# A hybrid layer with product-key experts: all picks of a group before their transposes, and longer leads in the written order

## The chip, the cores and the metric

The kernel runs on one core of a Trainium2 chip. The time is device microseconds (us) of one execution. Below, PE is the tensor engine (PEld its weight loads), DVE the vector engine, ACT the scalar engine, POOL the general engine, SP the engine that issues most DMAs.

## The reference

One layer on 1024 tokens of width 1024, in float32:

```python
h = rmsnorm(x, norm_mix_g)
hq, hf, hi, hg, cb, cc, ch, gates = split(h @ w_in)
# HGRN2: a gated linear recurrence, 8 heads x 64, chunks of 64 tokens
#   S_t = diag(f_t) S_(t-1) + k_t v_t^T ;  o_t = S_t^T q_t ;  k_t = 1 - f_t
y_a = rmsnorm_per_head(o) * hg_out_norm_g * silu(hg)
y_b = cb * causal_depthwise_conv3(cc * ch)
merged = sigmoid(g_a) * (y_a @ w_branch_hg) + sigmoid(g_b) * (y_b @ w_branch_conv)
x = x + merged @ w_out
# PEER: 8 heads, each the 16 best of 128 x 128 experts by two lists of 128 keys
q = rmsnorm(x) @ w_query
v1, i1 = top_k(q[:, :, 0] . keys1, 16);  v2, i2 = top_k(q[:, :, 1] . keys2, 16)
top_s, pos = top_k(v1 + v2, 16);  idx = (i1 * 128 + i2)[pos];  gate = softmax(top_s)
x = x + sum_k gate * gelu(peer_u[idx] . h) * peer_v[idx]
out = rmsnorm(x)
```

## The kernel before

The 1024 tokens are 8 tiles of 128, and the tiles are mixed in five groups: 0, 1, then 2 and 3, 4 and 5, 6 and 7. For each group `front` (L494) transposes the normalised input and makes the convolution branch, `recurrence` (L557) goes through four pairs of heads, `gates_a` and `gates_b` make the merge gates, and `post` (L606) merges, multiplies by `w_out`, takes the second norm (L646), transposes its result on PE (`transpose_whole`, L260, copied out by ACT at L261), multiplies by `w_query` (the loop with L251 and L665) and finds the best 16 keys of each half. `picks_of` (L685) then calls `pick` (L820) for each tile: the best 16 of the candidates (`top16`), the softmax, and the numbers of the experts (an equality, a product and a sum per head, L865, L867, L868).

The experts are computed in two ways. Tiles 0, 1, 6 and 7 fetch their rows of `peer_u` and `peer_v` one by one with indirect DMAs issued by POOL (L913); each row costs DVE one pass (L943 for u, L949 for v, called row operations below). Tiles 2 to 5 go through a dense phase, in which PE multiplies with all experts (L287, L290, L1068, L278 to L280; DVE L239, L1043, L1079): for these tiles `pick` ends with an integer conversion (L882) and three PE transposes (L886) whose results ACT copies out, and `all_gates` (L968) spreads the gates over all 16384 experts ahead of the dense phase (DVE L1007, L1010, PE L987, ACT L991, L1015; a *spread*).

The recurrence of one pair of heads: a scan on DVE (L573), differences of its levels on POOL (L704, L708), exponentials on ACT (L710), products on DVE (L718, L719), then in `chunks` (L724) for each tile 28 small matmuls of scores (L739, L741; *score matmuls*) with one transpose (L744), the masks on DVE (L749, L757), and two *state steps*, each with matmuls at L764, L768, L770 and the new state on DVE (L775). A matmul at L787 for the output norm ends a pair.

The written order of all this is decided ahead of time. `together` (L387) holds these generators and always runs the one that has done the smallest share of its total, by a clock that counts modelled matmul time; a `yield` with a number makes a generator sleep for that many units, so other generators' work is written ahead of what comes behind it. These numbers stand in one line (L67): LEV lies between the products and the score matmuls, GRAM between score matmuls and the first state step, STATE between state steps, NORM between the norm and its transposes, PICK between L882 and the transposes at L886. A scheduler then settles the order on each engine; on the chip each engine runs its list strictly in that order and waits on semaphores. So a `yield` costs no time by itself: it chooses what stands ahead of a wait.

The row operations enter by `paced`, one step of rows (two of u, two of v) each 7 units of that clock while the mixing goes on, and by `interleave` in the dense phase, which spreads the steps that are left over it.

Of the kernel before, what the change touches and what calls it, by code (L numbers as in the profile page):

```python
# [23 lines left out]
P = 128  # L24
# [39 lines left out]
T_GB, T_FIRST = 27, 40.0  # L64
ROW_STEPS, T_DENSE = 290, 1305.0

LEV, GRAM, STATE, MERGE, NORM, PICK, SPREAD, OUT = 11.55, 1.944, 0.864, 4.752, 3.24, 50.0, 2.592, 3.24  # L67


def zipped(a, b, every):  # L70
# [55 lines left out]
class Layer:  # L126
# [61 lines left out]
    def place_picks(self, q):  # L188

        r, M, at = self.ring, types.SimpleNamespace(), self.M.big[q]  # L190
        M.top_kb, M.topi_kb = at, at + 2
        M.pr, M.cu, M.fi, M.ci = r(at + 4, 1.625), r(at + 5.625, 1), r(at + 4, 1), r(at + 7.25, 1.625)
        M.cv, M.eq, M.tvp = r(at + 8.875, 1.625), r(at + 8.875, 1.625), r(at + 10.5, .5, 2)
        M.gt, M.pf, M.xf = r(at + 11.5, .5), r(at + 12, .5), r(at + 12.5, .5)
        M.xu, M.i12 = r(at + 13, 1), r(at + 14, 1)
        return M

    def place_dense(self):
# [486 lines left out]
    def picks_of(self, G):  # L685

        while self.posted < G.no:
            yield 1
        for t in range(G.n // P):
            yield from self.pick(G.n0 // P + t, G.top[:, t], G.topi[:, t], G.mem)  # L690
        self.picked = G.no

    def decays(self, qs, k, b):
# [126 lines left out]
    def pick(self, tile_no, top, topi, mem):  # L820

        nc = self.nc
# [22 lines left out]
        if for_gather:  # L845
            gate = self.picks.tile([P, HEADS, TOPK], F32, tag=f"gate{tile_no}", name="gate")
        else:
            gate = mem.gt.take([HEADS, TOPK])
# [22 lines left out]
        xf, gate = (z.rearrange("p h k -> p (h k)") for z in (xf, gate))  # L871
# [6 lines left out]
        xu, i12 = mem.xu.take([2, PICKS], U32), mem.i12.take([2, PICKS])  # L878
# [1 line left out]
        nc.vector.tensor_scalar(xu[:, 1], xu[:, 0], NKEYS - 1, None, op0=ALU.bitwise_and)  # L880
        nc.vector.tensor_scalar(xu[:, 0], xu[:, 0], 7, None, op0=ALU.logical_shift_right)
        nc.vector.tensor_copy(i12, xu)  # L882
        yield PICK
        ps = self.ps()
        for i, src in enumerate((i12[:, 1], i12[:, 0], gate)):
            self.tc.keep_in_program_order(nc.tensor.transpose(ps[:, i * P:(i + 1) * P], src, self.ident))  # L886

# [1 line left out]
        at = self.M.pt_kb + 2 * DENSE.index(tile_no)  # L889
        keys, gate, beyond = self.view(at, [P, 2, 2], F16), self.view(at + 1, [P]), self.view(at + 1.5, [P, 2], F16)  # L890
# [6 lines left out]
                                upper.unsqueeze(2).broadcast_to([P, P, 2]), op=ALU.subtract)  # L897
        pt = keys, gate, beyond
        self.pt[tile_no] = pt
        yield  # L900


    def gather(self, tiles):
# [290 lines left out]
```

## Time and profile before

| | before |
|---|---|
| median of 3 runs | 3154.16 us (3154.1 to 3157.51) |
| profiled execution | 3154.26 us, its span 3152.5 us |
| PE busy | 2844.1 us, 90% of the span |
| DVE busy | 2592.4 us, 82% |
| ACT busy | 1236.9 us, 39% |
| POOL busy | 1444.8 us, 46% |
| mean granted TensorE clock | 0.94 |

The span is the time from the first to the last instruction; the execution's time is 1.8 us longer. The shares are averages over stages: from 1850 us to the end lies the dense phase in full speed, before it the mixing.

### The profile page before, as it was taken

What the parts mean: (1) busy time and instruction counts of PE and PEld (TensorE: products, weight loads), DVE (VectorE), ACT (ScalarE), POOL (GpSimd) and SP (SyncE); (2) the same over time, 40 slices, a digit from 0 to 9 for tenths busy, and PEclk for the clock granted to TensorE, in tenths of its full rate; (3) what the DMA queues carried; (4) which work ended last, traced back from release to release, by engine and by line L of the source; (5) the groups of instructions that cost most, each with busy time, mean ns of one, the idle gap of its engine ahead of it and who ended that gap; (6) DMA issues with size and microseconds to landing.
All of it is one profiled execution on the core that took longest, in us unless ns stands there. A gap on an engine that the chain in (4) does not pass through costs nothing.

```text
span 3152.5 us, 45726 instructions
## 1 busy us (share of the span) xinstructions
PE 2844.1 (90%) x15988; PEld 2423.3 (77%) x15988; DVE 2592.4 (82%) x5706; ACT 1236.9 (39%) x2241; POOL 1444.8 (46%) x1328
## 2 busy tenths in 40 slices
PE   8899789998998988456686999999999999999998
PEld 7898678877887777345575878888888888888886
DVE  3347467887799979987879999998888989888888
ACT  3632633332333567356662333332333333333332
POOL 0102444466543632553625454555555546455442
PEclk9999799999999999777798999999999999999999
DMA  8588688989887897878798888999999989999986
GB/s 288 199 281 289 226 303 317 329 294 357 313 316 276 318 344 277 288 251 295 270 374 287 305 309 323 369 363 332 339 340 342 345 296 370 344 346 332 337 303 239
DMA packets 336135, 979.08 MB, mean 311 GB/s; under 512 B 30881, under 2 KB 107169, under 8 KB 333857
## 3 DMA queue, kind: packets, MB, share of 16 engines
q0 software_dynamic: 147456, 536.94, 47.4%
q1 hardware_dynamic: 188448, 439.23, 38.8%
q8 instruction: 126, 2.06, 0.2%
q14 instruction: 105, 0.85, 0.1%
HBM read 929.90 MB, written 46.14 MB: 310 GB/s over the span
## 4 chain that ended last, share of the span: by engine, by line
PE 56%; DVE 14%; ACT 6%; DMA 3%; issue 3%; POOL 3%; DVEq 0%; POOLq 0%; ACTq 0%
PE ps L1068 17%; PE ps L287 14%; PE ps L290 7%; PE ps L251 7%; DVE mem_g L949 3%; DVE mem_g L943 2%; PE ps L278 2%; PE ps L280 2%; PE ps L279 2%; PE ps L632 2%; ACT mem_y L1015 1%; ACT mem_a L991 1%; DMA mem_a<-in_peer_u,idx 1%; PE ps L739 1%; DVE mem_o L1007 1%
## 5 line engine op out<-in xcount | busy, mean ns | idle before, releaser
L251 PE MATMUL ps<-mem_h,mem_w 128*128 128x256 f32 (+1 forms) x4480 | 858.5, 350 | 17.2 <-ACT mem_h L261 11.3
L251 PEld LDWEIGHTS ps<-mem_h,mem_w 128*128 128x128 f32 x4480 | 741.9, 199 | 97.1 <-ACT mem_h L261 12.2
L913 POOL DMA_INDIRECT mem_g<-in_peer_v,idx x320 | 399.5, 1248 | 475.8 <-DVE mem_g L943 180.6
L913 POOL DMA_INDIRECT mem_g<-in_peer_u,idx x329 | 399.7, 1215 | 447.0 <-DVE mem_g L949 138.7
L1068 PE MATMUL ps<-mem_v,mem_ph 128*128 128x512 f32 x2304 | 567.2, 396 | 12.2 <-ACT mem_ph L238 12.2
L1068 PEld LDWEIGHTS ps<-mem_v,mem_ph 128*128 128x128 f32 x2304 | 433.3, 188 | 118.6 <-ACT mem_ph L238 13.1
L287 PE MATMUL ps<-mem_ht,mem_s 128*128 128x512 f32 x2048 | 510.1, 391 | 9.4 <-DVE mem_ht L239 7.3
L287 PEld LDWEIGHTS ps<-mem_ht,mem_s 128*128 128x128 f32 x2048 | 386.2, 189 | 92.5 <-DVE mem_ht L239 8.0
L943 DVE SCALAR_TENSOR_TENSOR mem_g<-mem_g 128x1024 f32<-128x1024 f32 x329 | 405.3, 1236 | 27.4 <-DMA mem_g<-in_peer_u,idx 25.2
L949 DVE SCALAR_TENSOR_TENSOR mem_g<-mem_g 128x1024 f32<-128x1024 f32 x320 | 412.3, 1288 | 17.7 <-DMA mem_g<-in_peer_v,idx 16.2
L238 ACT ACTIVATE mem_s<-mem_raw 128x512 fp32r<-128x512 f32 x256 | 161.4, 632 | 588.7 <-PE ps L287 555.7
L913 POOL DMA_INDIRECT mem_e<-in_peer_v,idx x150 | 196.3, 1309 | 193.1 <-DVE mem_g L949 167.3
L290 PE MATMUL ps<-mem_ht,mem_s 128*128 128x512 f32 x1024 | 275.6, 391 | 0.0
L913 POOL DMA_INDIRECT mem_e<-in_peer_u,idx x134 | 175.9, 1313 | 162.6 <-DVE mem_e L943 131.2
L239 DVE TENSOR_TENSOR mem_s<-mem_raw,mem_s 128x512 fp32r<-128x512 f32 x256 | 176.3, 691 | 72.7 <-PE ps L290 45.8
L290 PEld LDWEIGHTS ps<-mem_ht,mem_s 128*128 128x128 f32 x1024 | 193.3, 189 | 40.5
L238 ACT ACTIVATE mem_v<-mem_z 128x1024 fp32r<-128x1024 f32 x128 | 129.2, 1054 | 209.9 <-PE ps L280 196.3
L949 DVE SCALAR_TENSOR_TENSOR mem_g<-mem_e,mem_g 128x1024 f32<-128x1024 f32 x150 | 191.7, 1278 | 0.4
L704 POOL TENSOR_TENSOR mem_y<-mem_y 128x128 f32<-128x128 f32 (+1 forms) x120 | 59.9, 499 | 269.2 <-DVE mem_y L573 240.5
L1015 ACT ACTIVATE mem_y<-mem_o,mem_z 128x128 f16<-128x128 f16 x512 | 156.2, 391 | 51.0 <-DVE mem_o L1007 50.9
L943 DVE SCALAR_TENSOR_TENSOR mem_e<-mem_e,mem_g 128x1024 f32<-128x1024 f32 x134 | 163.1, 1219 | 5.6 <-DMA mem_e<-in_peer_u,idx 3.8
L239 DVE TENSOR_TENSOR mem_v<-mem_z,mem_v 128x1024 fp32r<-128x1024 f32 x128 | 153.1, 1217 | 0.0
(194 smaller groups left out, 4150.4 us busy)
## 6 DMA issues: line engine op xcount, KB each, us to landing
mem_w<-in_w_in SPq DMA_DIRECT2D x200, 512.0 KB
mem_raw<-in_peer_ut SPq DMA_DIRECT2D x128, 512.0 KB
mem_z<-in_peer_v SPq DMA_DIRECT2D x128, 512.0 KB
mem_w<-in_w_query SPq DMA_DIRECT2D x80, 512.0 KB
wd<-mem_a SPq DMA_DIRECT2D x16, 2048.0 KB
mem_z<-wd SPq DMA_DIRECT2D x32, 1024.0 KB
mem_w<-in_w_out SPq DMA_DIRECT2D x40, 512.0 KB
mem_w<-in_w_conv SPq DMA_DIRECT2D x40, 256.0 KB
```

The source lines that it names most:

```text
L238: self.nc.scalar.activation(hi, src, AF.Copy)
L239: self.nc.vector.tensor_tensor(lo, src, hi.bitcast(F32), op=ALU.subtract)
L251: self.nc.tensor.matmul(ps, w[:, kk, :], act[:, kk, :], start=kk == 0, stop=kk == k - 1)
L278: mm(ps, lh, rh, start=first, stop=False, **kw)
L279: mm(ps, lh, rl, start=False, stop=False, **kw)
L287: mm(ps, w[kk][0], act[part][:, kk, :], start=kk == part == 0, stop=False)
L290: mm(ps, w[j][1], act[0][:, j, :], start=False, stop=j == k - 1)
L913: nc.gpsimd.indirect_dma_start(out=r, out_offset=None, in_=a[table], in_offset=bass.IndirectOffsetOnAxis(ap=self.idx[t][:, k:k + 1], axis=0))
L943: nc.vector.scalar_tensor_tensor(u, u, 1.0, h2, op0=ALU.mult, op1=ALU.mult, accum_out=wt[:, k:k + 1])
L949: nc.vector.scalar_tensor_tensor(acc, v, wt[:, k:k + 1], acc, op0=ALU.mult, op1=ALU.add)
L1015: nc.scalar.activation(q[:, tk, 0, :], o[:, tk, 1, :], AF.Copy, scale=gate[:, tk:tk + 1])
L1068: nc.tensor.matmul(acc[t][hf], pp[c][i][:, tk], vp[c][:, k, 512 * hf:512 * hf + 512], start=c == 0 and i == 0 and k == 0, stop=c == NKEYS ...
```

## The change

The diff, without the lines around it:

```diff
-LEV, GRAM, STATE, MERGE, NORM, PICK, SPREAD, OUT = 11.55, 1.944, 0.864, 4.752, 3.24, 50.0, 2.592, 3.24
+LEV, GRAM, STATE, MERGE, NORM, PICK, SPREAD, OUT = 13.0, 3.0, 1.3, 4.752, 6.0, 40.0, 2.592, 3.24
...
-        M.gt, M.pf, M.xf = r(at + 11.5, .5), r(at + 12, .5), r(at + 12.5, .5)
-        M.xu, M.i12 = r(at + 13, 1), r(at + 14, 1)
+        M.gt, M.pf, M.xf = r((at + 11.5, at + 6.75), .5), r(at + 12, .5), r(at + 12.5, .5)
+        M.xu, M.i12 = r(at + 13, 1), r(at + 14, 1, 2)
...
         while self.posted < G.no:
             yield 1
+        late = []
         for t in range(G.n // P):
-            yield from self.pick(G.n0 // P + t, G.top[:, t], G.topi[:, t], G.mem)
+            late.append((yield from self.pick(G.n0 // P + t, G.top[:, t], G.topi[:, t], G.mem)))
+        for turn in filter(None, late):
+            yield PICK
+            turn()
+            yield
         self.picked = G.no
...
-        yield PICK
-        ps = self.ps()
+        return lambda: self.turned(tile_no, i12, gate)
+
+    def turned(self, tile_no, i12, gate):
+
+        nc, ps = self.nc, self.ps()
         for i, src in enumerate((i12[:, 1], i12[:, 0], gate)):
             self.tc.keep_in_program_order(nc.tensor.transpose(ps[:, i * P:(i + 1) * P], src, self.ident))
...
         self.pt[tile_no] = pt
-        yield
```

No instruction is added or removed but ACT's loads of its function tables, 187 instead of 192 by the two orders. For tiles 0, 1, 6 and 7 `pick` returns nothing, so the first part acts for tiles 2 to 5 alone; their converted numbers and their gates get a second buffer, since two tiles' now live at a time. Behind the change, lines from 690 on stand 5 to 7 lines lower. In the rows of an order below, `xN` counts instructions of the program; a matmul in fp32 stands twice in the trace where it has 256 columns (x8 here is x16 there).

PE around the norm of tiles 2 and 3 (787 us in the trace): L251 are weight blocks, L632 is `w_out`, L260 the transposes of the normalised tiles, L739/L741/L744 the first score matmuls of the next group (L744/L746/L749 behind the change). Before:

```order
L251 MATMUL ps<-mem_h_155,mem_w 128x256 x24
L632 MATMUL ps<-mem_w,mem_h_159 128x256 x8
L251 MATMUL ps<-mem_h_155,mem_w 128x256 x8
L260 MATMUL ps<-c_ident,mem_z 128x128 x8
L739 MATMUL ps<-mem_y 64x32 x6
L741 MATMUL ps<-mem_y 64x64
...
L744 MATMUL ps<-c_ident,mem_y 128x128
L260 MATMUL ps<-c_ident,mem_z 128x128 x8
L251 MATMUL ps<-mem_h_159,mem_w 128x256 x4
L764 MATMUL ps<-mem_y,st_119 128x64
```

and behind the change:

```order
L251 MATMUL ps<-mem_h_155,mem_w 128x256 x24
L632 MATMUL ps<-mem_w,mem_h_159 128x256 x8
L251 MATMUL ps<-mem_h_155,mem_w 128x256 x16
L251 MATMUL ps<-mem_yy,mem_w 128x256 x4
L744 MATMUL ps<-mem_y 64x32 x6
L746 MATMUL ps<-mem_y 64x64
...
L749 MATMUL ps<-c_ident,mem_y 128x128
L260 MATMUL ps<-c_ident,mem_z 128x128 x16
L769 MATMUL ps<-mem_y,st_119 128x64
L775 MATMUL ps<-mem_y 64x64 x2
```

Eight more weight matmuls, four of the convolution branch (mem_yy) and all 28 score matmuls with their transpose now stand ahead of the transposes of the norm, and the 16 transposes stand together.

PE around the transposes of tile 4's picks (L886 before, L894 behind the change). L770, L768 and L764 are state steps, L987 spreads (a LDWEIGHTS and a matmul each). Before:

```order
L987 MATMUL ps<-mem_y,mem_o 128x128
L770 MATMUL ps<-mem_y 64x64 x2
L768 MATMUL ps<-mem_y 64x64 x4
L764 MATMUL ps<-mem_y,st_119 128x64
L251 MATMUL ps<-mem_h_159,mem_w 128x256 x8
L770 MATMUL ps<-mem_y 64x64 x2
L764 MATMUL ps<-mem_y,st_120 128x64
L768 MATMUL ps<-mem_y 64x64 x4
L886 MATMUL ps<-c_ident,mem_z 128x128 x3
L251 MATMUL ps<-mem_h_159,mem_w 128x256 x8
L251 MATMUL ps<-mem_yy,mem_w 128x256 x4
```

and behind the change (L775, L773, L769 are the state steps' lines, L994 the spreads'):

```order
L994 MATMUL ps<-mem_y,mem_o 128x128
L251 MATMUL ps<-mem_h_159,mem_w 128x256 x8
L251 MATMUL ps<-mem_yy,mem_w 128x256 x4
L773 MATMUL ps<-mem_y 64x64 x4
L769 MATMUL ps<-mem_y,st_119 128x64
L773 MATMUL ps<-mem_y 64x64 x2
L894 MATMUL ps<-c_ident,mem_z 128x128 x3
L994 LDWEIGHTS mem_o
...
L994 MATMUL ps<-mem_y,mem_o 128x128
L775 MATMUL ps<-mem_y 64x64 x2
L251 MATMUL ps<-mem_h_159,mem_w 128x256 x8
```

Half of the state steps' matmuls and eight weight matmuls have moved from ahead of the transposes to behind them; sixteen spread matmuls that stood between the scores and these rows did the same.

DVE in the dense phase's first blocks, between the fifth and the sixth L1079 (L1086 behind the change), which takes a block's sums out of PSUM; L949 and L943 are row operations (L956, L950 behind). Before:

```order
L1079 TENSOR_TENSOR mem_z<-mem_z,ps 128x512
L949 SCALAR_TENSOR_TENSOR mem_g<-mem_e_12335,mem_g 128x1024
L239 TENSOR_TENSOR mem_ph<-mem_z,mem_ph 128x512
L867 TENSOR_TENSOR mem_z<-mem_z 128x800
L1079 TENSOR_TENSOR mem_z<-mem_z,ps 128x512
```

and behind the change:

```order
L1086 TENSOR_TENSOR mem_z<-mem_z,ps 128x512
L956 SCALAR_TENSOR_TENSOR mem_g<-mem_g 128x1024
L833 TENSOR_SCALAR mem_z<-mem_z 128x8x16
L817 MATCH_REPLACE rest<-mem_z 128x50
L821 MAX_INDEX mem_z<-mem_z 128x8
...
L950 SCALAR_TENSOR_TENSOR mem_g<-mem_g 128x1024
L854 TENSOR_TENSOR gate<-mem_z 128x128
L950 SCALAR_TENSOR_TENSOR mem_g<-mem_g 128x1024
L956 SCALAR_TENSOR_TENSOR mem_g<-mem_e_12351,mem_g 128x1024
L1086 TENSOR_TENSOR mem_z<-mem_z,ps 128x512
```

Between these two now stand 30 rows of the order instead of 3, with seven row operations instead of one and the search for the best 16 of tile 6 (L815 to L823) among them.

## Rows read from the trace of the kernel before

**Rows 1.** The page's head and its part 1: busy time, share, instructions.
```profile
span 3152.5 us, 45726 instructions
...
PE 2844.1 (90%) x15988; PEld 2423.3 (77%) x15988; DVE 2592.4 (82%) x5706; ACT 1236.9 (39%) x2241; POOL 1444.8 (46%) x1328
```

**Rows 2.** Windows; PE, PEld, DVE, ACT, POOL busy us, granted clock, DMA share, GB/s.
```profile
...
800.00:1300.00 500.00, 449.30 (x2874) 391.65 (x2873) 455.30 (x1397) 254.44 (x549) 221.70 (x213) 0.93 0.86 310
1300.00:1370.00 70.00, 8.14 (x61) 6.61 (x59) 61.65 (x150) 4.95 (x14) 43.63 (x33) 0.56 0.79 263
1370.00:1620.00 250.00, 180.25 (x1280) 154.63 (x1279) 202.63 (x353) 180.93 (x394) 119.74 (x105) 0.79 0.79 295
1620.00:1850.00 230.00, 201.86 (x929) 168.00 (x928) 216.12 (x654) 72.76 (x125) 106.18 (x79) 0.93 0.84 297
1850.00:3152.00 1302.00, 1288.64 (x5596) 1049.58 (x5595) 1159.64 (x1602) 407.92 (x598) 668.05 (x524) 1.00 0.92 333
```

**Rows 3.** PE's waits, 0 to 1800 us; total, times, longest us.
```profile
...
PE ps L886 <- DVE mem_z L814: 38.4, 1, 38.4
PE ps L768 <- DVE mem_y L757: 38.4, 7, 23.5
...
PE ps L886 <- DVE mem_y L757: 10.4, 1, 10.4
```

**Rows 4.** PE timeline at tile 4's transposes: start, us, what, [idle before <- releaser].
```profile
1367.89 0.87 PE L886 MATMUL ps<-c_ident,mem_z 128*128 128x128 f32 x3 [38.41 <-DVE mem_z L814]
1368.55 6.03 PE L251 MATMUL ps<-mem_h,mem_w 128*128 128x256 f32 x16
1374.42 1.89 PE L251 MATMUL ps<-mem_yy,mem_w 128*128 128x256 f32 x8
1376.15 1.06 PE L987 MATMUL ps<-mem_y,mem_o 128*128 128x128 f16 x16
```

**Rows 5.** DVE timeline, the end of tile 4's picks.
```profile
1366.28 1.26 DVE L949 SCALAR_TENSOR_TENSOR mem_g<-mem_g 128x1024 f32<-128x1024 f32 x1
1367.46 0.28 DVE L882 CAST mem_z<-mem_z 128x256 f32<-128x256 uint32 x1
```

**Rows 6.** PE timeline around the norm at 787 us.
```profile
770.85 3.62 PE L251 MATMUL ps<-mem_h,mem_w 128*128 128x256 f32 x16
...
786.96 1.94 PE L260 MATMUL ps<-c_ident,mem_z 128*128 128x128 f32 x8 [12.49 <-DVE mem_z L646]
788.83 1.51 PE L739 MATMUL ps<-mem_y 64*64 64x32 f32 x14
...
794.06 1.91 PE L260 MATMUL ps<-c_ident,mem_z 128*128 128x128 f32 x8
```

**Rows 7.** PE timeline, a state step of group 0.
```profile
156.88 0.66 PE L764 MATMUL ps<-mem_y,st 128*128 128x64 f32 x2 [0.77 <-DVE st L775]
```

**Rows 8.** PE timeline around the norm of tile 1.
```profile
461.16 1.04 PE L260 MATMUL ps<-c_ident,mem_z 128*128 128x128 f32 x8
473.18 3.35 PE L251 MATMUL ps<-mem_h,mem_w 128*128 128x128 f32 x11 [10.99 <-ACT mem_h L261]
```

**Rows 9.** PE timeline, the norm at 1120 us.
```profile
1120.18 3.65 PE L260 MATMUL ps<-c_ident,mem_z 128*128 128x128 f32 x16 [9.22 <-ACT mem_y L1015]
```

**Rows 10.** ACT by line: one of its table loads; busy, mean ns | idle before.
```profile
L540 ACT ACT_TABLE_LOAD x15 | 19.2, 1283 | 7.2 <-PE ps L251 7.0
```

**Rows 11.** PE timeline, the last norm.
```profile
1613.41 3.64 PE L260 MATMUL ps<-c_ident,mem_z 128*128 128x128 f32 x16 [11.91 <-DVE mem_z L646]
```

**Rows 12.** DVE timeline, the dense phase's first blocks.
```profile
1795.57 0.68 DVE L1079 TENSOR_TENSOR mem_z<-mem_z,ps 128x512 f32<-128x512 f32 x1
1798.45 0.68 DVE L1079 TENSOR_TENSOR mem_z<-mem_z,ps 128x512 f32<-128x512 f32 x1
```

**Rows 13.** PE timeline, the same blocks.
```profile
1802.10 1.98 PE L287 MATMUL ps<-mem_ht,mem_s 128*128 128x512 f32 x8
...
1846.93 3.00 PE L287 MATMUL ps<-mem_ht,mem_s 128*128 128x512 f32 x8 [2.07 <-DVE mem_z L1079]
```


## The prediction

> **What bounds it now.** I read the page first: PE is busy for 2844 of 3152 us, so at most 300 us could be won, and DVE is next with 82% [rows 1]. Shares over a whole span hide stages, so I asked for windows [rows 2]. From 1850 us on PE is busy for 1289 of 1302 us at a granted clock of 1.00. The change moves nothing there that PE waits for, so whatever happens earlier moves the start of this stage and with it the end: the question is how many microseconds PE's work ahead of 1850 us gains or loses.
>
> Ahead of that the picture changes twice. From 800 to 1300 us DVE is nearly full (455 of 500), PE 449. From 1300 to 1370 us PE is nearly idle (8 of 70 us) while DVE is busy for 62 of 70. From 1370 to 1620 us nobody is full: PE 180, DVE 203, ACT 181 of 250; that is a chain of short steps between three engines. Then DVE is full again (216 of 230).
>
> The list of PE's waits gives the single places [rows 3]: 38.4 us in one piece at the transposes of tile 4's picks, right behind a wait of 23.5 us in a state step. The timeline shows what ends the long one: the transposes start at 1367.89 [rows 4], and DVE's conversion L882, which makes their input, starts at 1367.46 behind row operations [rows 5]. The releaser named in the row, L814, is only the search that stands beside it.
>
> **The change, term by term.** No work is added, so each term is a wait that grows or shrinks because other work now stands ahead of it. A negative number is time gained. A weight step "W8" is 3.62 us (sixteen matmuls in the trace [rows 6]), a step of the convolution branch "Y4" 1.89 us and sixteen spreads 1.06 us [rows 4].
>
> 1. *The recurrence of group 0.* The state steps of its third pair now stand without weight blocks between them. The existing row of such a bare step waits 0.77 us for the state [rows 7]; four steps at that price, less what the blocks gain by standing earlier, give 0 to +6 (the upper end if the blocks are missed by a wait as well); I take +2.
>
> 2. *The norm of tile 1.* PE transposes at 461.16 and then waits 10.99 us for ACT's copies [rows 8]. Now W8 and Y4 stand ahead of the transposes, so 5.5 us of work fills what was idle: −5.5, between 0 (the copies move by as much) and −11.
>
> 3. *The norm of tiles 2 and 3.* PE waits 12.49 us at 786.96 for L646 [rows 6]. W8, Y4 and the 28 score matmuls move ahead: 3.62 + 1.89, and for the scores 5.2 us (788.83 to 794.06, the second half of the transposes). If the scores' inputs are late they only move; −5.5 to −12.5, and I take −8.5, with half of the scores covered.
>
> 4. *The norm at 1120 us* waits 9.22 us [rows 9]. The 28 scores and a few spreads now stand ahead of it: 0 to −9.2. DVE is nearly full there, so its norm ends no earlier and PE's gain must still be good for something; I take −3.
>
> 5. *Tile 4's transposes.* They still stand behind the same state step, and DVE's list has 82 instructions instead of 85 between the two things PE waits for. Both orders' instructions, at the mean durations of this trace, give DVE 986 and 985 us of work up to L882. The shorter PICK does not make DVE's result earlier. 0.
>
> 6. *Behind these transposes.* What stood ahead of the wait and was free there (W8, sixteen spreads, half of the state steps) now comes behind it: 1.06 + 3.62, or 6.03 for W8 at the speed it has just behind the wait [rows 4], + about 1 us for the states: +5.7 to +8.1. Against that, tile 5's conversion comes with 69 us of DVE work behind tile 4's instead of 86, so its wait of 10.4 us [rows 3] may go. Bounds −10.4 and +8.1; PE has 70 us of waits in this stage to take the moved work, so I take +4.
>
> 7. *ACT.* Five loads of its tables go, 1.283 us each in the trace [rows 10]. Three of them lie where ACT is half idle; two lie between tile 4's and tile 5's transposes, where ACT is part of the chain: −2.6 (0 to −6.4).
>
> 8. *The last norm* waits 11.91 us [rows 11]; the eight transposes of its second tile get sixteen or thirty-two more spreads ahead of them: −2 (0 to −4).
>
> 9. *The start of the dense phase.* The step of rows that comes earlier and the picks of tile 6 put seven row operations of 1.26 us [rows 5] and some 7 us of small searches between the fifth and the sixth L1079: about 16 us of DVE, where the trace has 2.9 us (1795.57 to 1798.45 [rows 12]). The sixth frees the sums that PE needs some blocks later. PE started that block at 1802.10, about 4 us behind the sixth, and already waits 2.07 us for an L1079 at 1846.93 [rows 13]. 13 us more, less a slack of 4 to 11: +2 to +9, and up to +12 if the row step ahead of the first one adds its 5 us; I take +6.
>
> The sum: 2 − 5.5 − 8.5 − 3 + 0 + 4 − 2.6 − 2 + 6 = −9.6. The profiled execution took 3154.26 us, the median of the runs is 3154.16, so the same: **3144.7, say 3145 us**. A measurement of this kernel can tell about 0.2%, or 6.3 us.
>
> **The skill beside two of these rows.** Behind the wait of 38 us the granted clock is low: 0.56 in that window [rows 2], and the first W8 takes 6.03 us where it takes 3.62 in running work [rows 4, 6]; behind the wait of 12.49 us eight transposes take 1.94 us against 1.04 at 461 us [rows 6, 8]. So a filled wait returns up to 1 or 2 us more than its length, and I leave that inside the bounds. The Trainium skill, "TensorE: Matmul & The Clock Gate", section "HAM oscillation — how this bites in real kernels", says that idle gaps put the array back to its lower clock and that each burst behind one starts cold. The rows agree; by that rule terms 2 to 4 would be a few us larger together, and term 6 would stay, since its wait does.
>
> The same notes, "ScalarE: Activation LUTs", section "What ACT_TABLE_LOAD costs", put a switch at about 2.66 us with its drain. By that, an estimate, term 7 would be −5.3 instead of −2.6 and the sum 3142. The trace shows the 1.283 us of the load alone; no row here shows the drain.
>
> **The rivals.**
>
> *A. The gains are swallowed (slower).* From 870 to 1368 us DVE has hardly a gap, and L882 decides when PE goes on. If DVE's list doesn't start this full stretch earlier because PE was earlier at 475 and 787 us, terms 2 to 4 vanish at 1367.89, and only the losses behind it remain: 3145 + 17 = 3162, and 3172 with the upper ends of terms 6 and 9. For it: DVE's 455 of 500 us, and the same 985 us of work ahead of L882. Against it: ahead of 870 us DVE is far from full and waits for PE's results, so it should move with PE. It decides if tile 4's transposes start at 1366 us or later.
>
> *B. Little of either (no change).* The gains reach 1368 us only in part and the dense phase's slack takes term 9: 3150 to 3158.
>
> *C. The losses are covered.* Tile 5's wait goes, the moved work of term 6 falls into the 70 us of waits, the slack covers term 9: 3154.3 − 5.5 − 8.5 − 3 − 2.6 − 2 + 2 = 3134.7, less up to 10.4: 3124 to 3135.
>
> *D. The words of the change hold for tile 4 too:* its wait of 38.4 us goes, to 3116 or below. For it only that the wait is there. Against it: the orders show the transposes behind the same two DVE results, at 0.1% of the same work.
>
> **How the numbers follow.** The forecast, 3138 to 3152 by the middle halves of its terms: 0.36, of which 0.08 fall within 0.2% of before. A: 0.29, of which 0.06 end within 0.2%. B: 0.17, of which 0.15 are within 0.2% and 0.02 slower. C: 0.13. D: 0.05. Faster by over 0.2%: 0.28 + 0.13 + 0.05 = 0.46; within 0.2%: 0.08 + 0.06 + 0.15 = 0.29; slower: 0.23 + 0.02 = 0.25. The range for 8 in 10 leaves out D, the lower part of C (0.05) and the part of A in which both late terms are at their upper ends and early work is lost too (0.1): 3126 to 3172.
>
> **What will show it.** Term 2: the wait behind the transposes of tile 1 is about 5 us instead of 11. Term 3: the wait for L646 near 780 us is 2 to 7 us, and the scores stand ahead of it. The sum of both is seen at tile 4's transposes: 1350 to 1357 us by the forecast, 1366 or later by A. Term 5: the wait there is again 30 to 40 us; if it is under 10, D holds. Term 6: the start of the last norm's transposes stands 240 to 252 us behind tile 4's (245.5 before); C if it is under 236. Term 9: the wait for an L1079 in the dense phase's first 100 us grows from 2 us to 4 to 12. I am wrong if the early waits shrink as said and DVE still reaches L882 at the old time, or if the dense phase starts with waits that the slack should have covered.

## The result, and the profile after

The changed kernel takes **3179.66 us** (median of 4 runs, 3176.55 to 3188.44), the kernel before 3154.62 us (4 runs, 3154.1 to 3157.51). The ratio is 1.0076, with a 95% interval of 1.006 to 1.0091: slower by 25 us, where 3145 us and a gain were forecast, and above the upper end of the range (3172 us). Two single runs of more than 4300 us, one of e9 and one of the kernel before beside e5 to e8, are left out of the figures below.

The profiled execution of the changed kernel took 3188.44 us, the slowest of its four, so its trace shows a loss of 34 us and not of 25. Lines behind the edits are shifted: the conversion L882 is now L887, the transposes L886 are L894, row operations L943 and L949 are L950 and L956, the spread's matmuls L987 are L994, its sum L1007 is L1014, and the dense phase's L1068 is L1075.

The page's head and its part 1, of the changed kernel (before: [rows 1]):

```profile
span 3186.7 us, 45716 instructions
...
PE 2863.6 (90%) x15988; PEld 2436.1 (76%) x15988; DVE 2591.9 (81%) x5706; ACT 1230.9 (39%) x2236; POOL 1446.3 (45%) x1328
```

DVE's work is the same (2591.9 and 2592.4 us), PE's number of matmuls too. The windows of [rows 2], in the changed kernel, with the same columns:

```profile
800.00:1300.00 500.00, 431.69 (x2680) 373.39 (x2680) 434.19 (x1366) 244.39 (x525) 205.94 (x205) 0.92 0.81 294
1300.00:1370.00 70.00, 17.86 (x143) 14.96 (x142) 59.93 (x93) 11.15 (x26) 44.10 (x33) 0.60 0.80 265
1370.00:1620.00 250.00, 174.47 (x1235) 149.66 (x1236) 207.06 (x411) 167.44 (x366) 127.30 (x110) 0.77 0.77 281
1620.00:1850.00 230.00, 187.11 (x897) 157.25 (x894) 208.94 (x648) 78.78 (x147) 94.95 (x76) 0.90 0.86 305
```

The first window is the place. DVE, which was busy for 455 of 500 us, is busy for 434, and PE falls from 449 to 432 with it: the stage that was full of vector work has got holes. The last two windows lose 6 and 15 us of PE's work as well. The places are these in PE's timeline (start, us, what, idle before and its releaser):

```profile
468.21 1.04 PE L260 MATMUL ps<-c_ident,mem_z 128*128 128x128 f32 x8
471.62 2.36 PE L744 MATMUL ps<-mem_y 64*64 64x32 f32 x14 [2.37 <-DVE mem_y L724]
...
779.56 0.91 PE L744 MATMUL ps<-mem_y 64*64 64x32 f32 x14
...
787.24 3.65 PE L260 MATMUL ps<-c_ident,mem_z 128*128 128x128 f32 x16 [4.56 <-DVE mem_z L646]
...
1383.66 0.87 PE L894 MATMUL ps<-c_ident,mem_z 128*128 128x128 f32 x3 [39.33 <-DVE mem_z L819]
...
1460.90 0.87 PE L894 MATMUL ps<-c_ident,mem_z 128*128 128x128 f32 x3 [19.74 <-DVE mem_z L887]
...
1639.47 1.94 PE L260 MATMUL ps<-c_ident,mem_z 128*128 128x128 f32 x8 [6.58 <-DVE mem_z L646]
...
1766.85 4.63 PE L1075 MATMUL ps<-mem_v,mem_ph 128*128 128x512 f32 x10 [18.05 <-ACT mem_ph L238]
```

Up to 790 us the change does what was forecast: the waits of 10.99 us [rows 8] and 12.49 us [rows 6] are 2.37 and 4.56. Then tile 4's transposes, which stood at 1367.89 [rows 4], stand at 1383.66, tile 5's wait has doubled, and the first matmul of the dense phase waits 18 us.

Five points in time, of PE in the profiled executions, divide the whole (us; starts, but for the last matmul; e1 is the first experiment, which has the four leads and not the rest):

| kernel | tile 4's transposes | last norm's transposes | first L1068 | end of the last matmul | span |
|---|---|---|---|---|---|
| before | 1367.9 | 1613.4 | 1732.9 | 3138.6 | 3152.5 |
| after | 1383.7 | 1639.5 | 1766.8 | 3168.8 | 3186.7 |
| after − before | +15.8 | +26.1 | +33.9 | +30.2 | +34.2 |
| e1 | 1357.6 | 1606.6 | 1718.6 | 3127.1 | 3141.1 |
| after − e1 | +26.1 | +32.9 | +48.2 | +41.7 | +45.6 |

### The profile page after: what moved, and what is told of

The parts are those of the page before. It is cut to its first block, busy times and chain, and to the rows that moved or that the text cites. A ratio compares the mean times of both kernels' runs of the same rounds, so it can differ in the third digit from the quotient of the medians.

```text
span 3186.7 us, 45716 instructions
## 1 busy us (share of the span) xinstructions
PE 2863.6 (90%) x15988; PEld 2436.1 (76%) x15988; DVE 2591.9 (81%) x5706; ACT 1230.9 (39%) x2236; POOL 1446.3 (45%) x1328
## 3 DMA queue, kind: packets, MB, share of 16 engines
q1 hardware_dynamic: 188448, 439.23, 38.4%
## 4 chain that ended last, share of the span: by engine, by line
PE 67%; DVE 13%; ACT 7%; DMA 6%; issue 4%; POOL 3%; SPq 0%; DVEq 0%; POOLq 0%; ACTq 0%
PE ps L1075 17%; PE ps L251 15%; PE ps L287 14%; PE ps L290 7%; PE ps L632 3%; DVE mem_g L956 2%; PE ps L280 2%; PE ps L278 2%; PE ps L279 2%; PE ps L744 2%; DMA mem_g<-in_peer_u,idx 2%; DVE mem_g L950 2%; DMA mem_g<-in_peer_v,idx 1%; DMA wd<-mem_a 1%; POOL mem_g L920 1%
## 5 line engine op out<-in xcount | busy, mean ns | idle before, releaser
L251 PE MATMUL ps<-mem_h,mem_w 128*128 128x256 f32 (+1 forms) x4480 | 865.1, 352 | 7.7 <-ACT mem_h L261 2.3
L251 PEld LDWEIGHTS ps<-mem_h,mem_w 128*128 128x128 f32 x4480 | 748.2, 200 | 90.7 <-ACT mem_a L998 3.7
L920 POOL DMA_INDIRECT mem_g<-in_peer_u,idx x330 | 407.5, 1235 | 438.3 <-DVE mem_g L956 131.5
L1075 PE MATMUL ps<-mem_v,mem_ph 128*128 128x512 f32 x2304 | 567.3, 396 | 18.5 <-ACT mem_ph L238 18.5
L1075 PEld LDWEIGHTS ps<-mem_v,mem_ph 128*128 128x128 f32 x2304 | 433.3, 188 | 124.9 <-ACT mem_ph L238 19.3
L950 DVE SCALAR_TENSOR_TENSOR mem_g<-mem_g 128x1024 f32<-128x1024 f32 x330 | 404.7, 1231 | 33.5 <-DMA mem_g<-in_peer_u,idx 29.3
L956 DVE SCALAR_TENSOR_TENSOR mem_g<-mem_g 128x1024 f32<-128x1024 f32 x321 | 417.5, 1301 | 12.3 <-DMA mem_g<-in_peer_v,idx 11.3
L956 DVE SCALAR_TENSOR_TENSOR mem_g<-mem_e,mem_g 128x1024 f32<-128x1024 f32 x148 | 189.4, 1280 | 0.6
L950 DVE SCALAR_TENSOR_TENSOR mem_e<-mem_e,mem_g 128x1024 f32<-128x1024 f32 x132 | 160.6, 1219 | 0.4 <-issue 0.3
```

The source lines that it names most:

```text
L251: self.nc.tensor.matmul(ps, w[:, kk, :], act[:, kk, :], start=kk == 0, stop=kk == k - 1)
L920: nc.gpsimd.indirect_dma_start(out=r, out_offset=None, in_=a[table], in_offset=bass.IndirectOffsetOnAxis(ap=self.idx[t][:, k:k + 1], axis=0))
L950: nc.vector.scalar_tensor_tensor(u, u, 1.0, h2, op0=ALU.mult, op1=ALU.mult, accum_out=wt[:, k:k + 1])
L956: nc.vector.scalar_tensor_tensor(acc, v, wt[:, k:k + 1], acc, op0=ALU.mult, op1=ALU.add)
L1075: nc.tensor.matmul(acc[t][hf], pp[c][i][:, tk], vp[c][:, k, 512 * hf:512 * hf + 512], start=c == 0 and i == 0 and k == 0, stop=c == NKEYS ...
```

## The experiments

Ratios are to the kernel before, run on the same chip, with their 95% interval. They differ from the quotient of the two medians by about 0.1% (e2: 1.0079, where 3177.13 to 3156.15 is 1.0066), so a difference of 4 us between two experiments says nothing.

### Which part of the change is it

**e1: the four leads alone.**

```diff
-LEV, GRAM, STATE, MERGE, NORM, PICK, ... = 11.55, 1.944, 0.864, 4.752, 3.24, 50.0, ...
+LEV, GRAM, STATE, MERGE, NORM, PICK, ... = 13.0, 3.0, 1.3, 4.752, 6.0, 50.0, ...
```

> The four longer leads alone (LEV, GRAM, STATE, NORM), the picks as before. Theory L, the leads are the loss (they fill PE's early waits with work that is then missing between the spreads and in the last group's recurrence): 3174 to 3185 us. Theory P, the picks are the loss (both tiles' picks in one piece, the transposes at another place): 3143 to 3155 us, with the early waits at the norms of tile 1 and of tiles 2 and 3 shrunk as in the changed kernel.

3141.2 us, ratio 0.9952 [0.9937, 0.9967]. That is just under the range of theory P and far from that of L: the leads alone give what the prediction gave to the whole change.

**e2: the picks alone**, the changed kernel with the four old leads (PICK stays 40).

> The picks part alone (all picks of a group first, PICK 40), the four leads as before. Theory L: 3150 to 3160 us. Theory P: 3170 to 3185 us, and the stretch from tile 3's transposes to the last group's first output norm takes about 58 us instead of 37.

3177.13 us, 1.0079 [1.0062, 1.0096]. So the picks part costs 21 us by itself (25 by the ratio), and 38 us on top of the leads (3179.7 against 3141.2). The stretch named in the expectation, from tile 3's transposes to the last group's first output norm (L787), takes 51.2 us here and 57.7 in the changed kernel, against 36.6 before and 36.8 in e1. So some 20 us of the loss lie in it.

**e3 and e4: the leads in one half of the program each.** e3 has them in the recurrences of the groups 0 to 3 and at the norms of the groups 0 to 2, e4 in the last recurrence and at the last two norms.

```diff
+    def leads(self, no):
+        return LEADS[no < 4]        # e4: LEADS[no > 3]
...
-        yield NORM
+        yield self.leads(G.no + 1)[3]
```

> The longer leads only in the recurrences of groups 0 to 3 and the norms of groups 0 to 2, picks as before. Theory L with the harm done in the last group: 3138 to 3150 us, since the early gain of about 14 us stays. Theory L with the harm done by the early leads (what they fill is missing later): 3165 to 3185 us. Theory P: 3140 to 3150 us.

> The longer leads only in the last group's recurrence and in the norms of groups 3 and 4, picks as before. Theory L with the harm in the last group: 3165 to 3185 us. Theory L with the harm by the early leads, and theory P: 3150 to 3160 us.

e3 3139.34 us, 0.9951 [0.9934, 0.9968]; e4 3152.44 us, 0.9991 [0.998, 1.0002]. The gain is in the first half; the longer leads at 1120 us and at the last norm bring nothing that can be told.

**e10, e11, e15: which lead.** e10 changes only NORM (to 6.0), e15 takes it to 9.0, e11 changes only LEV, GRAM and STATE.

> Only the longer lead behind the norm (NORM 6.0), all else as before. If terms 2 and 3 of the prediction were due to it (the work ahead of the norms' transposes): 3139 to 3148 us, most of the 15 us that the four leads gained. If the leads of the recurrence carry the gain: 3150 to 3158 us.

> Only the longer leads of the recurrence (LEV, GRAM, STATE), NORM as before. If NORM carried the gain: 3150 to 3160 us. If these carry it: 3138 to 3148 us.

> Only the lead behind the norm, 9.0 in place of 3.24 (6.0 gave 3140 us). If more work ahead of the norms' transposes still covers a wait: 3130 to 3138 us. If their waits are covered or the norm's own work then comes late: 3138 to 3152 us.

e10 3140.2 us, 0.9937 [0.9921, 0.9954]; e11 3150.12 us, 0.9971 [0.996, 0.9983]; e15 3138.69 us, 0.9938 [0.9921, 0.9956]. The lead behind the norm is enough for the whole gain (17 us by the medians), and more of it gives nothing more. The leads of the recurrence gain 7 us alone and nothing beside NORM, so the two do not add. The traces show why e11 gains less: PE's last matmul ends at 3127.4 us in it, as in e1 (3127.1) and e10 (3127.2), but its last row operation starts only at 3138.9, behind PE's end; in e1 it starts at 3112.9.

### Where the picks part costs

**e5 and e6: leads, and picks found together in one group only**: tiles 2 and 3 in e5, tiles 4 and 5 in e6 (there `G.no != 3`).

```diff
         for t in range(G.n // P):
+            if G.no != 2 and late[-1]: yield 50.0; late.pop()(); yield    # behind each pick
```

> The longer leads, and the picks of tiles 2 and 3 found together (PICK 40) while tiles 4 and 5 are treated as before. Theory P1: the harm is that tile 3's picks follow tile 2's with none of the 34 row operations that stood between them, so the row fetches stop for some 30 us and the same rows and DVE's work come back later, where DVE is the bound: this kernel has about 24 us of the loss, 3160 to 3170 us. Theory P2: the harm is where the transposes of tiles 4 and 5 stand: 3138 to 3148 us.

> The longer leads, and the picks of tiles 4 and 5 found together (PICK 40) while tiles 2 and 3 are treated as before. Theory P1: about 15 us of loss or less, 3145 to 3157 us. Theory P2: nearly the whole loss, 3168 to 3182 us.

e5 3168.85 us, 1.004 [1.0025, 1.0055]; e6 3151.18 us, 0.9983 [0.9973, 0.9994]. Against e1 that is 28 us for tiles 2 and 3, and 10 us for tiles 4 and 5. Together they come to the 38 us of the picks part, as theory P1 has it.

**e7: leads and PICK 40, each tile's transposes ahead of the next pick, as before. e8: the whole change, and a sleep of 50 units between a group's two picks.**

```diff
# e7: the line of e1 with PICK 40.0. e8:
         for t in range(G.n // P):
+            if late and late[-1]: yield 50.0
             late.append((yield from self.pick(...)))
```

> The longer leads and PICK 40, but each tile's transposes again ahead of the next tile's picks. Theory P1: 3138 to 3150 us, since 37 row operations stand between the two conversions. Theory that the shorter PICK is the loss: 3160 to 3180 us.

> The whole change, but a sleep of 50 units between the picks of a group's two tiles, so that 23 row operations stand between the conversions of tiles 2 and 3 again; the transposes still come after both. Theory P1: most of the loss goes, 3140 to 3158 us. Theory P2: 3168 to 3185 us.

e7 3172.11 us, 1.0056 [1.0039, 1.0073]; e8 3149.94 us, 0.9977 [0.9967, 0.9987]. With its two picks apart the changed kernel loses only 9 of the 38 us. That points at the second pick's place, but e8 moves more than that: the norm at 1120 us stands at 1082, the last norm's transposes at 1573.8, 33 us ahead of e1's, and from the last norm to the first L1068 it then takes 149.9 us against 111.0. e7 misses P1's range: the shorter PICK alone costs 31 us, as the rival theory had it. Its loss lies at another place, the start of the dense phase (below); up to tile 4's transposes it is 7 us behind e1, where e5 is 23. No run has the picks together with a PICK of 50, so what the shorter PICK costs within the whole change stays open.

### What happens ahead of tile 4

In the changed kernel tile 3's search stands directly behind tile 2's. DVE's timeline shows the end of both:

```profile
1002.68 0.29 DVE L887 CAST mem_z<-mem_z 128x256 f32<-128x256 uint32 x1
...
1048.85 0.60 DVE L887 CAST mem_z<-mem_z 128x256 f32<-128x256 uint32 x1
1049.38 1.75 DVE L950 SCALAR_TENSOR_TENSOR mem_g<-mem_g 128x1024 f32<-128x1024 f32 x1
```

The second conversion stood at 1109.8 before and stands at 1106.3 in e1. Between the two conversions there is no row operation now, where there were 34 before. What stops with them is seen in two windows (columns as in [rows 2]) of e1, and then of the changed kernel:

```profile
960.00:1240.00 280.00, 241.16 (x1472) 209.22 (x1471) 255.39 (x687) 166.82 (x375) 113.96 (x109) 0.92 0.84 303
1000.00:1030.00 30.00, 20.96 (x104) 17.87 (x105) 29.74 (x89) 20.12 (x50) 17.41 (x11) 0.83 0.66 219
```

```profile
960.00:1240.00 280.00, 231.75 (x1391) 200.31 (x1390) 230.93 (x616) 149.87 (x338) 104.97 (x100) 0.90 0.76 278
1000.00:1030.00 30.00, 21.03 (x125) 17.56 (x126) 23.31 (x97) 23.31 (x52) 0.20 (x1) 0.88 0.19 54
```

From 1000 to 1030 us POOL issues next to nothing (0.20 us against 17.41) and the transfers fall from 219 to 54 GB/s. DVE itself is busy for 23.31 of these 30 us, in e1 for 29.74: the search's steps wait, and no row operation stands between them to fill the waits. The rows come later instead, in the stretch in which the search work is now missing between the spreads. There DVE waits too. Its waits from 1000 to 1240 us, of the changed kernel (total, times, longest):

```profile
DVE mem_o L1014 <- PE ps L994: 16.0, 5, 6.9
```

and of e1:

```profile
DVE mem_o L1007 <- PE ps L987: 7.3, 4, 3.0
```

The chain of the changed kernel there has one long link, a spread's buffer that is written out before ACT can fill it again (the chain of the kernel before has one of 7.65 us, at 1269.67):

```profile
1173.31 10.89 DMA wd<-mem_a
```

All of it together, from the norm of tiles 2 and 3 (the end of its last L646) to tile 4's conversion, worked out from every record of DVE in that stretch (idle: nothing runs on DVE; a row operation on `peer_u` leaves two records and is counted once). The last column is the shorter stretch within it, from tile 3's transposes to the last group's first output norm:

| kernel | us | DVE busy | DVE idle | row operations | from tile 3's transposes |
|---|---|---|---|---|---|
| before | 579.5 | 523.0 | 56.4 | 189 | 36.6 |
| e1 | 570.3 | 518.3 | 52.1 | 188 | 36.8 |
| after | 595.0 | 515.0 | 80.0 | 187 | 57.7 |
| e2 (picks alone) | 585.3 | 516.6 | 68.7 | 184 | 51.2 |
| e5 (tiles 2, 3) | 593.3 | 522.8 | 70.5 | 190 | 56.8 |
| e6 (tiles 4, 5) | 565.0 | 513.6 | 51.5 | 185 | 36.8 |
| e7 (PICK 40) | 577.8 | 527.6 | 50.2 | 194 | 36.3 |
| e8 (apart) | 562.4 | 512.1 | 50.3 | 187 | other order |
| e13 (rows put back, below) | 583.4 | 515.8 | 67.6 | 189 | 38.4 |

The work differs by 3 us between e1 and after, the idle time by 28; in e2 the idle time grows by 12 over before, in e5 by 18 over e1. e6, e7 and e8, in which tile 3's picks stand apart from tile 2's, have no such idle time.

**e9 and e13: the whole change, with the rows put back into tile 3's search** (a row step in each of its six breaks, the next six paced steps left out). If the stopped row stream is the cause, the idle time must go.

```diff
...
+            found = self.pick(...)
+            late.append((yield from (self.with_rows(found) if (G.no, t) == (2, 1) else found)))
```

> The whole change, but one row step is written into each of the six breaks of tile 3's pick (26 row operations between the two conversions instead of none), and the next six paced steps are left out in return, so that tile 4's conversion has 347 row operations ahead of it as against 345. The picks still follow each other at once. If the loss before tile 4 comes from the stop of the row stream (no fetches by POOL for 30 us, transfers that crowd later): DVE's idle time from 960 to 1240 us falls from 49 to about 30 us and the time to 3150 to 3165 us. If it comes from the picks' work being gone as a filler for DVE, however the rows are spread: 3172 to 3185 us.

> The kernel of the ninth run once more, for its profile. If the picks' work as a filler for DVE is what is missing: DVE's idle time from 960 to 1240 us is 40 to 50 us although row operations stand inside tile 3's pick and POOL fetches rows between 1000 and 1030 us. If the stop of the row stream were the cause, it would be 25 to 35 us.

e9 3172.66 us (median of four runs), 1.0047 [1.003, 1.0064]. The trace is from e13, one more run of the same kernel: 3170.01 us. Its windows:

```profile
960.00:1240.00 280.00, 229.42 (x1433) 200.16 (x1433) 244.64 (x661) 161.22 (x363) 114.44 (x107) 0.92 0.81 291
1000.00:1030.00 30.00, 17.83 (x114) 15.30 (x113) 28.88 (x80) 22.27 (x48) 12.20 (x11) 0.83 0.63 204
```

The transfers are back at 204 GB/s, and DVE is busy for 28.88 of the 30 us. The stretch from tile 3's transposes, which had grown from 36.8 to 57.7 us, takes 38.4: that growth goes when row operations stand in the search. Tile 4's transposes stand at 1366.7 instead of 1383.7 (e1: 1357.6), and DVE's idle time in the long stretch is 67.6 us instead of 80.0 (e1: 52.1). By these single traces the stopped rows are 17 of 26 us by the transposes and 12 of 28 by the idle time.

The marks set beforehand do not agree. From 960 to 1240 us DVE is idle for 35.4 us (49.1 in the changed kernel, 24.6 in e1), at the edge of the 25 to 35 of the stopped rows. But e9's time lies in the range of the other theory, 3172 to 3185. In the two traces the 17 us are kept to the end (spans of 3168.2 and 3186.7); by the medians e9 is only 7 us faster than the changed kernel, whose trace is its slowest run. So the stopped rows are shown as a cause of the lost time ahead of tile 4, and how much of the whole loss they make is not shown. The rest I take for the search work that is missing as filler, but no run separates that from the later place of the spreads.

### The start of the dense phase

From the end of the last norm to the first L1068 it takes 118.4 us before, 111.0 in e1, 126.3 after, 131.0 in e7 and 127.9 in e13. DVE's busy time in this stretch is 106.1, 98.1, 112.6 and 113.3 us in the first four. The row operations in it number 38, 35, 43 and 42. PE's timeline at that matmul, in e1 and then in e7:

```profile
1718.64 4.60 PE L1068 MATMUL ps<-mem_v,mem_ph 128*128 128x512 f32 x12 [7.16 <-DMA mem_g<-in_peer_u,idx]
```

```profile
1745.76 1.65 PE L1068 MATMUL ps<-mem_v,mem_ph 128*128 128x512 f32 x3 [20.68 <-ACT mem_ph L238]
```

e7 reaches the last norm 7 us behind e1 (1613.8 against 1606.6) and this matmul 27 us behind it: most of its loss is here.

**e12 and e14: the leads, with other row steps from the last norm to the dense phase**: none in e12, at twice the distance in e14 (`normed` is set behind the last norm).

```diff
-        while not self.stop:
+        while not self.stop and not self.normed:              # e12
...
-            yield ROW_STEP
+            yield 2 * ROW_STEP if self.normed else ROW_STEP   # e14
```

> The four longer leads, and no more row steps written from the last norm on until the dense phase, whose pacing takes them over. If the start of the dense phase is bound by DVE's work ahead of the first product with peer_v (111 us of work between the last norm and that product with only the leads, 126 in the whole change): that stretch shrinks by 8 to 25 us and the time is 3118 to 3134 us. If it is bound by PE's own work or by a transfer: 3136 to 3146 us.

> The four longer leads, and from the last norm to the dense phase every row step at twice the distance (about half of the 41 row operations that the twelfth run moved). With all of them moved the dense phase started 25 us earlier and the rows ended 44 us behind PE; with the leads alone they end 14 us ahead of it. If the two ends balance: the dense phase starts 8 to 14 us earlier, the rows end about with PE, and the time is 3126 to 3136 us. If the rows decide already: 3140 to 3160 us.

e12 3171.5 us, 1.0047 [1.0033, 1.0061]; e14 **3129.87 us, 0.9926 [0.9905, 0.9947]**, the lowest of all, though its interval overlaps those of e1, e10 and e15. The stretch takes 95.1 us in e12 (no row operation) and 99.6 in e14 (20 of them), against 111.0 in e1 (35): DVE's rows do set when the dense phase begins. The stretch of e12 shrinks as expected, the time misses both ranges: rows that are left out have to be done later. The end of e12 as a window:

```profile
3100.00:3165.00 65.00, 1.71 (x8) 1.04 (x6) 58.17 (x100) 5.75 (x10) 27.03 (x26) 0.53 0.72 273
```

PE is through at 3101.7, 25 us ahead of e1, and DVE is at work for 60 us more: the last row operation ends at 3147.4, 46 us behind PE's end, where in e1 it ends at 3114.2, 13 us ahead of PE's end. e14 lies between: PE ends at 3099.7, the last row operation ends at 3107.7, and the span is 3125.5. The stretch ahead of the dense phase in e14, as a window:

```profile
1596.70:1696.30 99.60, 91.86 (x469) 80.14 (x468) 85.98 (x398) 36.86 (x68) 26.31 (x24) 0.93 0.83 299
```

PE is busy for 92 of 100 us there; in the changed kernel it does the same 92 us of work in 126:

```profile
1640.50:1766.80 126.30, 92.17 (x453) 79.57 (x451) 112.63 (x430) 33.49 (x67) 53.32 (x45) 0.85 0.90 325
```

## Why the prediction was wrong

**Terms 2 and 3 (the early norms, −14) were right in mechanism and, as a sum, in size.** The sum of the two is seen at the second pair of matmuls at L787 (now L792) behind 800 us, which in the kernel before start at 899.5. (Half of the scores make term 3 −8.1 and not −8.5.) In the changed kernel's timeline of PE:

```profile
885.32 0.70 PE L792 MATMUL ps<-mem_y,c_headmean 128*128 128x256 f32 x2 [0.53 <-ACT mem_y L789]
```

That is 14.2 us earlier. The waits are 2.37 and 4.56 us, where "about 5" and "2 to 7" were forecast, and the scores stand ahead of the second one. How the 14 us divide is not shown: the pair of L792 at 756.6 stands where it stood before. e1 is 16.0 us earlier at the same pair and 11.4 at the end of its span.

**Term 5 failed: "tile 4's transposes, 0".** It compared DVE's work up to L882 (986 and 985 us) and concluded that the time would be the same. The work was the same, within 3 us of e1's. But an engine's result comes after its work *and its idle time*, and the same instructions in another order had 28 us more of it. The prediction took it that DVE "has hardly a gap" from 870 to 1368 us. The trace has 40 us of gaps there (busy for 458 of 498), and from 870 to tile 4's transposes in the changed kernel 67:

```profile
870.00:1368.00 498.00, 387.86 (x2498) 338.05 (x2499) 458.15 (x1371) 231.12 (x510) 227.03 (x206) 0.88 0.85 302
```

```profile
870.00:1383.00 513.00, 381.06 (x2340) 328.29 (x2339) 446.38 (x1324) 229.35 (x504) 222.11 (x205) 0.85 0.80 289
```

I had seen in the order that the two searches moved together, and priced the move by its instructions alone. The size is +26 against e1, or +16 against before, where the leads' 10 us are taken off. Terms 1 to 5 forecast −15 at this place, so 31 of the 44 us by which this trace misses the sum are here.

**Rival A's mark came true, in the main for another reason.** It put tile 4's transposes at 1366 or later, because early gains would be swallowed by a full DVE. They stand at 1383.66. In e1, whose searches are as before, they stand at 1357.62 (forecast 1350 to 1357): of the 16.0 us gained at the pair of L787, 10.3 are left, so a part was swallowed. In e10, with NORM alone, that pair is 20.3 us earlier and tile 4's transposes stand at 1368.62, where they stood before: there A held up to this place, and the gain comes behind it (the last norm's transposes at 1599.2, before 1613.4), by a way that I did not follow. D was false, as argued: the wait at these transposes is 39.33 us, 38.4 before [rows 3].

**Term 6 (behind the transposes, +4) was too small.** From tile 4's transposes to the last norm's it takes 255.8 us (240 to 252 forecast), before 245.5, in e1 249.0. Tile 5's wait, which I thought might go, is 19.74 instead of 10.4. e6, in which only tiles 4 and 5 are picked together, takes 261.3 there, so two searches in one piece cost time here too.

**Term 9 (+6) was near in size and at the wrong place.** The stretch ahead of the dense phase is 7.9 us longer than before (126.3 and 118.4), but the loss is ahead of its first matmul (18.05 us of wait, 11.26 before), not between the fifth and the sixth L1079. The 16 us of DVE's work that were forecast between these two came as priced (now L1086):

```profile
1830.03 0.67 DVE L1086 TENSOR_TENSOR mem_z<-mem_z,ps 128x512 f32<-128x512 f32 x1
...
1846.02 0.69 DVE L1086 TENSOR_TENSOR mem_z<-mem_z,ps 128x512 f32<-128x512 f32 x1
```

What failed is the slack of "4 to 11": PE did not wait for the sixth, and behind the first matmul its waits up to 1870 us are 1.2 us in all. And the loss is not a matter of tile 6's searches alone: e7 has it from PICK alone, with seven row operations more in the stretch than e1.

**The rest.** Term 1 (+2) can't be told: tile 0's norm ends at 203.4 us, before at 201.5, but at 204.9 in e4, whose leads are the old ones there; all leads of the recurrence, alone, gain 7 us (e11). Terms 4 and 8 are lost in e4's −4 us, which can't be told from none; the last norm's wait itself shrank from 11.91 [rows 11] to 6.58. Term 7, the five table loads, was in no experiment by itself. In the trace of the kernel before, the median time from the end of ACT's instruction ahead of a load to the start of the one behind it is 1.31 us. The longer price, with a drain, that the Trainium skill gives, "ScalarE: Activation LUTs", section "What ACT_TABLE_LOAD costs", is not seen in it. The clock behind a shortened wait stayed low: with 4.56 us of wait instead of 12.49, sixteen transposes still take 3.65 us at a granted clock of 0.50 (the level of 1.2 GHz), and eight behind running work take 1.04 (468.21) at 1.00 (2.4 GHz). The Trainium skill, "TensorE: Matmul & The Clock Gate", section "HAM oscillation — how this bites in real kernels", says that each burst behind such a gap starts cold; the trace agrees. So the shortened wait brought nothing back by the clock.

What stays open: why PICK 40 in e7 brings the row steps together ahead of the dense phase, which is a matter of the written order that I did not follow generator by generator, and the part of the idle time that the rows don't explain. The trace of a single execution has a spread of its own: e1, e12 and e14 are the same program up to the last norm, and tile 4's transposes stand at 1357.6, 1354.0 and 1348.4 in them. So a difference of under 10 us at one such place proves little. The argument is carried by the 26 us at tile 4's transposes, which e5 repeats (1381.0, 23 us behind e1), and by the stretch of 37 us, which grows by 20 in both kernels, by 15 in e2 and by under 2 in e6, e7 and e13.

## What to carry to other kernels

When instructions are moved on a busy engine, equal work up to a result is no reason for an equal time: ask which of the moved pieces filled waits of others, what streams (here rows that POOL fetches and DVE consumes) stand still while one long piece runs, what will fill the waits within that piece, and what will fill the stretch that the piece has left. Split a change by its parts before judging it: here one number, the lead behind the norm, was worth 17 us, and the rest hid it. And the rate of a background stream can be wrong both ways: with some half of the rows in a stretch that waits for DVE the ratio was 0.9926, against 0.9952 in e1 (a difference that the intervals leave open), and with none of them 30 us were lost.

## What the runs showed of the hardware

- In this kernel the stream of gathered rows does not run ahead while DVE does other work: from 1002.7 to 1049.4 us DVE runs tile 3's search without a row operation, and from 1000 to 1030 the transfers fall to 54 GB/s (219 in e1 in the same 30 us).
- Rows that were put off were not made up in this kernel's dense phase: with the 35 row operations of e1's stretch put off, the last one of e12 ended 33 us later than in e1 (3147.4 and 3114.2), although the phase had begun 18 us earlier.
